# Four groups of z as two 512-wide seven-product units in the front of a hybrid decoder layer

## The chip, the cores and the metric

The kernel runs on one core of a Trainium2 chip. The metric is the device time of one execution in microseconds; lower is better. The core's engines are called PE (TensorE, matmuls), DVE (VectorE), ACT (ScalarE), POOL (GpSimd) and SP (SyncE, which issues the DMAs here). They run side by side, each through its own queue in order, and wait for one another through semaphores.

## The reference

One layer over 1024 tokens of width 1024:

```python
h = rms_norm(x, norm_w)
proj = h @ w_in
q, k, v, z_a, xbc, z_s, dt_raw, gate_logits = jnp.split(proj, SPLIT_POINTS, axis=-1)
...
y_a = diff_attention(...)                  # 8 heads, two softmax maps per head
y_a = y_a * jax.nn.silu(z_a)
xbc = jax.nn.silu(causal_depthwise_conv(xbc, conv_w, conv_b))
...
y_s = ssd_chunked(...)                     # 32 heads in 4 groups, chunks of 128
y_s = gated_group_rms_norm(y_s, z_s, ssd_norm_w)   # group g uses silu of z_s[:, 512 g : 512 g + 512]
merged = sigmoid(g_a) * (y_a @ w_proj_attn) + sigmoid(g_s) * (y_s @ w_proj_ssd)
x = x + (merged @ w_out)
```

The change is in the front: the parts of `h @ w_in` that give z_s (2048 columns, called z below, four groups of 512), xBC (the conv's input, 3072 columns, blocks c0 to c23) and the first gates (g0 to g11).

## The kernel before

**Arithmetic.** All large matmuls are in float32r with each operand split into a high and a low part (h into hH and hL, a weight tile into its two halves w[:, 0] and w[:, 1]). Each product is three matmuls, hi x hi, hi x lo, lo x hi (`steps3`, which calls `mm`, L205). A split is a copy on ACT (`act`, L231) and a subtraction on DVE or POOL (`tt`, L239).

**Seven products.** Most blocks of the projection are multiplied in 2 x 2 halves with seven products instead of eight. With h's halves and weights' halves, the sums of h's parts are the forms t1 to t4 (beside the plain b11, b21, b22), and the sums of the weights' parts are made on POOL. `ORDER` names the seven as (form of h, number of the product): b11 1, t2 6, b21 2, t3 7, t1 5, t4 4, b22 3. Products 1 and 2 go to one PSUM bank, the others to two more; between them DVE and ACT carry partial sums (ct is the copy of product 1, u6 and u7 are that copy plus products 6 and 7).

- `front_pair` does this for two conv blocks or two gates (kinds c and g): weights are stationary, the moving operand is 128 x 512, the banks are fX, fY, fZ. Its step (`conv_step`, `gate_step`, `front_sum`) copies product 1 as fc, makes fu and fW, and sends the result on to conv or gate.
- `tok_unit` does it for one group of z: here the tokens are stationary and the moving operand is a 128 x 256 tile of weights (`tok_w`, `tok_splits`: the tiles rawt, wt, s3), so its matmuls write halves of the banks tx, ty, tz, two of each.
- `ssd_proj_z` makes one group of z plainly, 512 wide. z0 is made this way (`PLAIN`); it runs first, while the tokens' tiles of h come in. `z_evac` applies silu and stores z in DRAM (z_d).
- `form_evac` makes the forms of a token tile (r11, r21 from hH + hL, b12 and b22 copied in `h_evac`), and splits them into sixteen tiles ft, all four forms for a tile after each other. Every product that reads a form waits until all forms of all tiles are made (`("formed", t)`).

**Weights.** `w_loads` issues the loads (raw, rawf, rawt, rawp) in the order of `wlist`, `w_splits` splits them into w, wt or wp; `pair_splits` forms the sums for `front_pair`. For the last product (w_out) `out_sums` makes the sums of the weights' parts beforehand and keeps them in DRAM (wf_d).

**What sets the order.** The source is a set of generators under a planner (`Plan`). It keeps a clock of its own from fixed costs for each operation, and emits instructions in the order that this clock gives; the order on each engine is thus fixed when the kernel is built. `bulk` is the main line, TensorE's large blocks in the order of `FRONT_ORDER`; the other tasks (`ssd_all`, `prepare`, the evacuations) insert their instructions between. `PACE` and `SLOW` are the planner's distances between chunks of the SSD scan. After the front come attention's projections and heads (pma, sc, av, with SSD chunks between), the remaining gates (pg), the products with w_proj (px, py, pz; their forms f0b, f0t, f1b ... are loaded from DRAM in `fill`, their weights as rawp), and the product with w_out (po).

Of the kernel before, what the change touches and what calls it, by code (L numbers as in the profile page):

```python
# [142 lines left out]
def tile_hybrid_layer(ctx: ExitStack, tc: tile.TileContext, x, norm_w, w_in, q_norm_w, k_norm_w,  # L143
# [215 lines left out]
    FPAIRS = [i for i in ORDER1 if i[0] in "cgazv" and i not in PLAIN]  # L359
# [5 lines left out]
    def tok_w(c0):  # L365
        return tuple(w_in[kh * 512 + kp * 256:kh * 512 + kp * 256 + 256, c0 + r * 256:c0 + r * 256 + 256]
                     .rearrange("(k p) c -> p k c", p=P) for kp in range(2) for kh in range(2) for r in range(2))

    PAIR_C = {"c": C_XBC, "g": C_GATE, "a": C_ZA}
    TOK_C = {"z": C_ZS, "v": C_V}  # L370
    for kind, i in ORDER1:
        if kind in PAIR_C:
            wlist.append(pair_w(w_in, 0, PAIR_C[kind] + i * P))
        elif kind in TOK_C and (kind, i) not in PLAIN:
            wlist.append(tok_w(TOK_C[kind] + i * 512))
        elif kind != "setup":
            wlist += att_w(i) if kind == "h" else wide_w(w_in, C_ZS + i * 512) if kind == "z" else block_w(w_in, KB, C_DT, SH)
# [19 lines left out]
    def w_loads(lo, hi):  # L397
        for i in range(lo, hi):
# [15 lines left out]
            if isinstance(wlist[i], tuple) and len(wlist[i]) == 8:  # L414
                ks = yield from pl.get(raws, 4)
                raw = [rpool.tile([P, 2, 256], F32, tag="raw", name=f"rawt{i}{q}") for q in range(4)]
                at = [load(raw[q], wlist[i][q]) for q in range(4)]
                km = yield from pl.get(mids, 4)
                raw += [midt([P, 2, 256], name=f"rawt{i}{q}") for q in range(4, 8)]
                at += [load(raw[q], wlist[i][q]) for q in range(4, 8)]  # L420
                raw_of[i] = (raw, ks, km, at)
                continue
            while i >= len(wlist) - NFIN and ("filled" not in ready or ready.get("out_sums", INF) > pl.t):
                yield pl.t + 0.5
            k = yield from pl.get(raws)
# [24 lines left out]
    def w_splits():  # L450
        for i in range(len(wlist)):
# [5 lines left out]
            if isinstance(wlist[i], list):  # L457
                yield from pair_splits(*raw_of.pop(i), "G" if i < NFRONT else "V")
                continue
            if isinstance(wlist[i], tuple) and len(wlist[i]) == 8:  # L460
                yield from tok_splits(*raw_of.pop(i))
                continue
# [14 lines left out]
            t = tt(lo, raw, hi, ALU.subtract, t, "G" if NW <= i < len(wlist) - NFIN and i % WPOOL == 0 else "V")  # L477
# [5 lines left out]
    def pair_splits(raw, ks, at, eng):  # L483
# [30 lines left out]
        raws.give(ks[0], max(t, t4))  # L514
        t22 = yield from split(a22, at[1], eng)
        t = yield from split(a12, t4, eng)
        raws.give(ks[2], t)
        raws.give(ks[3], max(t, t22))

    def tok_splits(raw, ks, km, at):  # L520

        a11, a21, a12, a22 = [[raw[q], raw[4 + q]] for q in range(4)]
        kt = yield from pl.get(mids, 2)
        s3 = [midt([P, 2, 256], name="s3") for _ in range(2)]

        def split(src, ts, eng):
            done = []
            for kp in range(2):
                k = yield from pl.get(ws)
                n = made[0]  # L530
                made[0] += 1
                wt = wpool.tile([P, 2, 2, 256], F32R, tag="w", name=f"wt{n}")
                yield ts[kp]
                t = act(wt[:, 0], src[kp], AF.Copy, ts[kp])
                yield t
                t = tt(wt[:, 1], src[kp], wt[:, 0], ALU.subtract, t, eng)
                wts[n], w_at[n], w_slot[n] = wt, t, k
                done.append(t)
            return done

        t0 = [max(at[0:4]), max(at[4:8])]
        t3, t1, t2, t4 = [], [], [], []
        for kp in range(2):
            yield t0[kp]
            t3.append(tt(s3[kp], a11[kp], a21[kp], ALU.subtract, t0[kp], "G"))
            t1.append(tt(a21[kp], a21[kp], a22[kp], ALU.add, t0[kp], "G"))
        u11 = yield from split(a11, t0, "V")
        for kp in range(2):
            t2.append(tt(a11[kp], a21[kp], a11[kp], ALU.subtract, max(t1[kp], u11[kp]), "G"))
        yield from split(a11, t2, "V")  # L550
        u12 = yield from split(a12, t0, "V")
        for kp in range(2):
            t4.append(tt(a12[kp], a12[kp], a11[kp], ALU.subtract, max(t2[kp], u12[kp]), "G"))
        raws.give(ks[0], t4[0])
        mids.give(km[0], t4[1])
        t = yield from split(s3, t3, "G")
        for kp in range(2):
            mids.give(kt[kp], t[kp])
        t = yield from split(a21, t1, "V")
        raws.give(ks[1], t[0])  # L560
        mids.give(km[1], t[1])
        t = yield from split(a22, t0, "G")
        raws.give(ks[3], t[0])
        mids.give(km[3], t[1])
        t = yield from split(a12, t4, "G")
        raws.give(ks[2], t[0])
        mids.give(km[2], t[1])
# [96 lines left out]
    def load_x(t):  # L664
# [626 lines left out]
    def tok_step(kind, g, p, b, bank, cell):  # L1291
# [4 lines left out]
        def out(src, o, k, at, free):  # L1296
# [5 lines left out]
            if free:  # L1302
                trs.give(kb, at)
# [892 lines left out]
```

## Time and profile before

| what | value |
|---|---|
| median of 3 runs (lowest to highest) | 1588.59 us (1586.92 to 1589.97) |
| profiled execution | 1586.5 us |
| its span | 1584.8 us |
| granted clock | 0.999 |
| PE busy | 1564.0 us, 8386 instructions |
| DVE, ACT, POOL busy | 1153.5, 939.0, 787.8 us |
| DMA | 247.56 MB, mean 156 GB/s |

The span is the stretch from the first to the last instruction of the profiled execution. A stretch such as 40 to 80 is in microseconds from its start. The front takes the first 580 us or so, attention lasts to about 1210, the last gates to 1260, the products to 1500, and w_out the rest. In rows of groups the columns are line, engine, operation, out<-in with shape and count, then busy us and mean ns of one, then the idle time before it and who ended it. In the chain of waits the columns are start, length, and what ran.

### The profile page before, as it was taken

To read this page: it belongs to the slowest core of one execution; us is meant where nothing else is said; L and a number is where in the kernel's file an instruction comes from. 1 tells how busy PE (TensorE), PEld (TensorE's weight loads), DVE (VectorE), ACT (ScalarE), POOL (GpSimd) and SP (SyncE) were. 2 spreads that over 40 slices of the span, in tenths; PEclk is the share of its full clock that TensorE was granted. 3 is DMA by queue.
4 is the path that set the end of the run, shared out by engine and by line. 5 is a ranking of instruction groups with operands and counts; after the bars stand their busy time and mean duration, and the time that the engine had idled before them with its cause. 6 is when DMAs were issued, how large, how long until landed. Compare 5 with 4: busy or idle time off the path is not lost.

```text
span 1584.8 us, 25484 instructions
## 1 busy us (share of the span) xinstructions
PE 1564.0 (99%) x8386; PEld 1330.4 (84%) x8386; DVE 1153.5 (73%) x2104; ACT 939.0 (59%) x2267; POOL 787.8 (50%) x909
## 2 busy tenths in 40 slices
PE   8999999999999999999999999999999999999999
PEld 6898889888988888888888888888888878888887
DVE  7967664777567666877777788776566677898985
ACT  8544456665475466777787777686566554443350
POOL 3554455554654533546594646445747664322005
PEclk9999999999999999999999999999999999999999
DMA  5233344345343461415273442324426787898846
GB/s 183 94 110 87 120 153 127 100 134 169 104 137 118 144 196 45 127 54 159 84 239 115 144 117 88 105 73 131 166 89 226 237 302 239 273 318 277 305 139 219
DMA packets 236006, 247.56 MB, mean 156 GB/s; under 512 B 15959, under 2 KB 168288, under 8 KB 235874
## 3 DMA queue, kind: packets, MB, share of 16 engines
q1 hardware_dynamic: 235870, 245.94, 48.5%
q8 instruction: 66, 1.08, 0.3%
q14 instruction: 66, 0.54, 0.1%
q10 hardware_dynamic: 4, 0.00, 0.0%
HBM read 172.35 MB, written 73.53 MB: 155 GB/s over the span
## 4 chain that ended last, share of the span: by engine, by line
PE 71%; ACT 4%; POOL 2%; DVE 1%; DMA 1%; issue 1%; SPq 0%; DVEq 0%; POOLq 0%; ACTq 0%
PE pma L205 18%; PE py L205 6%; PE sc L205 4%; PE pO L205 4%; PE av L205 4%; PE px L205 4%; PE pz L205 4%; PE fYc L205 3%; PE pg L205 3%; PE fXc L205 2%; PE pa L214 2%; PE fZc L205 2%; PE fYg L205 2%; PE poz L205 1%; PE fZg L205 1%; PE poy L205 1%
## 5 line engine op out<-in xcount | busy, mean ns | idle before, releaser
L205 PE MATMUL pma<-w,hH 128*128 128x512 f32 x1024 | 342.3, 403 | 1.9 <-POOL w L239 1.7
L205 PEld LDWEIGHTS pma<-w,hH 128*128 128x128 f32 x1024 | 187.9, 189 | 35.1 <-POOL w L239 2.1
L205 PE MATMUL pma<-w,hL 128*128 128x512 f32 x512 | 206.9, 404 | 0.0
L239 POOL TENSOR_TENSOR rawf<-rawf,rawf 128x512 f32<-128x512 f32 x54 | 70.5, 1306 | 116.4 <-DVE wp L239 42.9
L231 ACT ACTIVATE p<-p,nm 128x256 f32<-128x256 f32 (+7 forms) x128 | 98.7, 774 | 26.9 <-DVE nm L941 21.5
L205 PEld LDWEIGHTS pma<-w,hL 128*128 128x128 f32 x512 | 96.6, 189 | 16.0
L205 PE MATMUL fYc<-ft,wp 128*128 128x512 f32 x432 | 105.0, 390 | 0.0
L231 ACT ACTIVATE w<-raw 128x512 fp32r<-128x512 f32 (+1 forms) x110 | 67.4, 626 | 49.0 <-DMA raw<-wf_d 12.8
L205 PEld LDWEIGHTS fYc<-ft,wp 128*128 128x128 f32 x432 | 80.9, 188 | 16.7
L231 ACT ACTIVATE wp<-rawf 128x512 fp32r<-128x512 f32 x108 | 64.8, 624 | 44.2 <-POOL rawf L239 19.7
L231 ACT ACTIVATE wp<-rawp 128x512 fp32r<-128x512 f32 x72 | 44.1, 627 | 76.7 <-POOL rawp L239 18.7
L231 ACT ACTIVATE ab<-ab,nac 128x128 f32<-128x128 f32 x256 | 78.5, 397 | 7.0 <-POOL ab L1450 6.8
L239 DVE TENSOR_TENSOR w<-raw,w 128x512 fp32r<-128x512 f32 (+1 forms) x85 | 68.2, 816 | 18.0 <-ACT w L231 17.6
L239 POOL TENSOR_TENSOR rawp<-rawp,rawp 128x512 f32<-128x512 f32 x36 | 54.4, 1528 | 52.0 <-DVE wp L239 43.7
L941 DVE CUSTOM_DVE_ANT_0 p<-sc,maskb 128x512 f32<-128x512 f32 (+3 forms) x128 | 72.3, 583 | 7.9 <-PE sc L205 7.1
L205 PEld LDWEIGHTS av<-v,at 128*128 128x128 f32 x576 | 72.5, 191 | 4.9 <-ACT at L231 1.3
L271 POOL TENSOR_TENSOR rs<-rs,mhalf 128x4 f32<-128x4 f32 (+1 forms) x71 | 73.3, 1033 | 5.9
L205 PE MATMUL av<-v,at 128*128 128x128 f32 x576 | 74.7, 275 | 0.5 <-ACT at L231 0.5
L973 POOL TENSOR_TENSOR rec<-s,mone 128x1 f32<-128x1 f32 x64 | 35.7, 560 | 74.8 <-ACT p L231 74.7
L205 PE MATMUL sc<-kk,qh 128*128 128x512 f32 (+2 forms) x192 | 66.7, 353 | 0.6 <-ACT ch L231 0.4
L239 DVE TENSOR_TENSOR wp<-rawf,wp 128x512 fp32r<-128x512 f32 x72 | 56.5, 798 | 14.8 <-ACT wp L231 14.8
L205 PE MATMUL fXc<-hH,wp 128*128 128x512 f32 x192 | 63.9, 392 | 0.0
(383 smaller groups left out, 4585.6 us busy)
## 6 DMA issues: line engine op xcount, KB each, us to landing
raw<-in_w_in_dram SPq DMA_DIRECT2D x80, 256.0 KB, 3.6
rawf<-in_w_in_dram SPq DMA_DIRECT2D x72, 256.0 KB, 3.4
ab<-act_d SPq DMA_DIRECT2D x32, 512.0 KB, 4.2
cv_d<-cv SPq DMA_DIRECT2D x48, 256.0 KB, 2.3
t_d<-ts SPq DMA_DIRECT2D x24, 512.0 KB, 2.7
xr<-cv_d SPq DMA_DIRECT2D x32, 256.0 KB, 3.5
zc<-z_d SPq DMA_DIRECT2D x32, 256.0 KB, 3.4
ys_d<-xdt SPq DMA_DIRECT2D x32, 256.0 KB, 2.5
```

Of the source, the lines that this page charges most:

```text
L205: nc.tensor.matmul(o, lhsT=lhsT, rhs=rhs, start=start, stop=stop, **kw)
L214: nc.tensor.transpose(out=o, in_=i, identity=ident if idn is None else idn)
L231: nc.scalar.activation(o, i, f, **kw)
L239: (nc.vector if eng == "V" else nc.gpsimd).tensor_tensor(out=o, in0=a, in1=b, op=op)
L271: nc.gpsimd.tensor_tensor(out=dst, in0=dst, in1=mhalf[:, 0:cols], op=ALU.pow)
L941: nc.vector.tensor_tensor_reduce(out=p[:, j:e], in0=sc[i][:, 0:e - j], in1=maskb[:, S - n + j:S - n + e], scale=-1.0, scalar=nms[i - 1] if ...
L973: nc.gpsimd.tensor_tensor(out=rec, in0=sums[1], in1=mone, op=ALU.pow)
```

## The change

- **z in two units of two groups.** `z_first` ("y0", "y1") computes, 512 wide and plainly, the token tiles 0 to 3 of groups 0 and 2 (products 1 and 2). After half of the sum ACT copies the bank (zc) and the copy goes to DRAM (zc_d); PE then adds the second half into the same bank. `z_part` ("z06", "z17": unit, product) does one of the five remaining products over four token tiles with 512-wide moving weights (banks pz); its partial sums (zu, zv) are loaded from DRAM and stored back, unless the next block of the order is a part of the same unit. The parts stand between other blocks.
- **Weight sums in DRAM.** `weight_sums` makes the four sums of a unit's weights on POOL from tiles os and stores them in wf_d, at the planner's times `ZSUMS`; the loads of z's parts read them from there, and wait until they are stored (`gate`). It also serves w_out in place of `out_sums`.
- **Four gates begun apart.** "e6", "e0", "e4", "e2" (`gate_first`) do products 1 and 2 of a gate pair (its first block, the first half of the tokens): half of the sum, copy by ACT (gc, kept in gc_d), the other half. The pair's remaining five products come later in the order `REST`, with the copy loaded as fc.
- **Forms one by one.** `form_evac` makes t2 for all token tiles, then t3 and t1, then t4; a product waits for its own form only (`formed`). b12 and b22 lie in one large tile (b2).
- **Numbers.** PACE 19.5 (19), SLOW 32 (40), POOL takes every third weight split only from i = 48 (`NEARLY`) and not from 9; the order of the front is another.

In all the program has 7280 large matmuls of the projections' kind in place of 7808 (1008 of 256 columns fall away, 480 of 512 come), 2145 DVE instructions in place of 2106, 2044 on ACT in place of 2038, 911 on POOL in place of 914, and SP issues 1068 DMAs in place of 916.

```diff
-PACE = 19
-FRONT, SLOW = 12, 40.0
-FRONT_ORDER = "z0 d0 z1 c16 c20 g0 c0 c2 g2 z2 c4 c6 g4 c18 c22 g6 z3 c8 c10 g8 c12 c14 g10"
-PLAIN = (("z", 0),)
+PACE = 19.5
+FRONT = 12
+SLOW = 32.0
+FRONT_ORDER = "y0 e6 y1 e0 e4 c6 e2 d0 c20 z06 c16 z07 z05 g0 c2 z04 c0 z16 z03 g2 z17 z15 z14 c4 z13 c8 g8 c14 g6 c22 g10 c12 g4 c10 c18"
+REST = (("t2", 6), ("b22", 3), ("t3", 7), ("t1", 5), ("t4", 4))
+ZSUMS = (75.0, 182.0, 11.0)
 WPOOL = 3
+NEARLY = 48
...
+    wf_d = dram.tile([12, 2, P, S], F32, name="wf_d")
+    gc_d = dram.tile([2048, 512], F32, name="gc_d")
+    zc_d = dram.tile([2, 2, 512, 512], F32, name="zc_d")
...
+    def blocks_w(src, c0, sums, p, kb):
+        if p in (1, 2, 4):
+            i, j = {1: (0, 0), 2: (1, 0), 4: (1, 1)}[p]
+            return src[(i * 4 + kb) * P:(i * 4 + kb + 1) * P, c0 + j * 512:c0 + (j + 1) * 512]
+        j, h = {6: (0, 0), 7: (0, 1), 3: (1, 0), 5: (1, 1)}[p]
+        return wf_d[sums * 4 + kb, j][:, h * 512:(h + 1) * 512]
...
+            while i in gate and ready.get(gate[i], INF) > pl.t:
+                yield pl.t + 0.2
...
-            t = tt(lo, raw, hi, ALU.subtract, t, "G" if NW <= i < len(wlist) - NFIN and i % WPOOL == 0 else "V")
+            t = tt(lo, raw, hi, ALU.subtract, t, "G" if NEARLY <= i < len(wlist) - NFIN and i % WPOOL == 0 else "V")
...
+    def formed(f, ts=range(4, NT)):
+        while any(("formed", f, t) not in ready for t in ts):
+            yield pl.t + 0.2
+        at = max(ready["formed", f, t] for t in ts)
+        if at > pl.t:
+            yield at
...
-                while any(("formed", t) not in ready for t in range(4, NT)):
-                    yield pl.t + 0.2
-                at = max(ready["formed", t] for t in range(4, NT))
-                if at > pl.t:
-                    yield at
+                yield from formed(f)
...
+    def gate_first(b):
+        ids = w_next(2)
+        k = yield from pl.get(trs, first=True)
+        pm = mmt(f"pe{b}")
+        for half in range(2):
+            yield from w_need(ids[half])
+            while half and ("g", b) not in g_c:
+                yield pl.t + 0.1
+            for kb in range(half * 4, half * 4 + 4):
+                yield from steps3(pm, blk(ids, kb), (hH[:, kb, 0:512], hL[:, kb, 0:512]), kb == 0, kb % 4 == 3, skip_group_check=True)
+            w_done(ids[half])
+            if half:
+                pl.spawn(gate_evac(b, 0, pm, k), pe_done())
+            else:
+                pl.spawn(gate_copy(b, pm), pe_done())
...
+    def gate_copy(b, pm):
+        at = pe_done()
+        km = yield from pl.get(mids)
+        c = midt(name=f"gc{b}")
+        at = act(c, pm, AF.Copy, at)
+        g_c["g", b] = at
+        yield at
+        g_c["g", b] = at = load(gc_d[b * P:(b + 1) * P], c, at)
+        mids.give(km, at)
...
+    def z_first(pr):
+        ids = w_next(KB)
+        for ts in (((0, 1), (2, 3)) if pr else ((0,), (1,), (2, 3))):
+            pms = []
+            for t in ts:
                 k = yield from pl.get(trs, first=True)
+                pms.append((mmt(f"pmz{pr}{t}"), k))
+            for half in range(2):
+                for t, (pm, k) in zip(ts, pms):
+                    while half and (pr, t) not in z_c:
                         yield pl.t + 0.1
+                    for kb in range(half * 4, half * 4 + 4):
+                        yield from w_need(ids[kb])
+                        while (t, half) not in h_at:
+                            yield pl.t + 0.1
+                        while h_at[t, half] > pl.t:
+                            yield h_at[t, half]
+                        yield from steps3(pm, hblk(kb, t), wide(ids[kb]), kb == 0, kb % 4 == 3, skip_group_check=True)
+                        if t == 3:
+                            w_done(ids[kb])
+                    pl.spawn(z_evac(2 * pr, t, pm, k, False) if half else z_copy(pr, t, pm), pe_done())
...
+    def z_copy(pr, t, pm):
         at = pe_done()
+        km = yield from pl.get(mids)
+        c = midt(name=f"zc{pr}{t}")
+        at = act(c, pm, AF.Copy, at)
+        z_c[pr, t] = at
+        yield at
+        z_keep(pr, 0, t, c, km, at, False)
...
+    def z_part(pr, p, keep):
+        f, ids = FORM_OF[p], w_next(4)
+        for t in range(4):
+            k = yield from pl.get(trs, first=True)
+            pm = trt(f"pz{p}{pr}{t}")
+            if f[0] == "t":
+                yield from formed(f, (4 + t,))
+            us = {}
+            pl.spawn(z_fetch(pr, p, t, us))
+            for kb in range(4):
+                yield from w_need(ids[kb])
+                yield from steps3(pm, [a[:, t * P:(t + 1) * P] for a in front_form(f, kb)], wide(ids[kb]), kb == 0, kb == 3)
+                if t == 3:
+                    w_done(ids[kb])
+            pl.spawn(z_step(pr, p, t, pm, k, us, keep), pe_done())
...
+    def z_step(pr, p, t, pm, k, us, keep):
+        at = pe_done()
+        while len(us) < 1 + (p == 5):
+            yield pl.t + 0.1
+        yield max([at] + [u[2] for u in us.values()])
+        at = pl.t
+        if p == 6:
+            c, km = us[0][0:2]
+            at = tt(c, c, pm, ALU.add, at)
+            trs.give(k, at)
             yield at
+            z_keep(pr, 0, t, c, km, at, keep)
...
+    def weight_sums(n, src, c0, at=0.0):
+        yield at
+        for kb in range(4):
+            ks = yield from pl.get(mids, 4)
+            a, b = [[midt(name=f"os{n}{kb}{j}{i}") for i in range(2)] for j in range(2)]
+            t = max(load((a, b)[j][i], src[(j * 4 + kb) * P:(j * 4 + kb + 1) * P, c0 + i * 512:c0 + i * 512 + 512])
+                    for j in range(2) for i in range(2))
+            yield t
+            for p, x, k, o, y, z, op in ((5, b[1], 3, b[1], b[1], a[1], ALU.add), (7, a[1], 1, a[1], a[0], a[1], ALU.subtract),
+                                         (6, a[0], 0, a[0], b[1], a[0], ALU.subtract), (3, b[0], 2, b[0], b[0], a[0], ALU.subtract)):
+                yield from pl.room("G")
+                t = tt(o, y, z, op, t, "G")
+                pl.spawn(sum_store(n, kb, p, x, ks[k], t))
+                if p == 3:
+                    ready["summed", n, kb] = t
+                t -= HOP
...
-        for kind, i in ORDER1:
+        step = {"y": z_first, "h": att_proj, "e": gate_first}
+        for i in range(2):
+            pl.spawn(weight_sums(i, w_in, C_ZS + i * 1024, ZSUMS[i]))
```

Three places show how the order moves. On PE in the startup (ph are transposes of x, pmz the banks of z's token tiles; a w is one weight tile) there stands before, at the middle of the first tile's sum:

```order
L214 MATMUL ph_234<-ident,x_142 128x128 [waits DVE_49]
L214 MATMUL ph_234<-ident,x_142 128x128 x3
L205 MATMUL pmz_144<-w_172,hH 128x512
L205 MATMUL pmz_144<-w_172,hL 128x512
L205 MATMUL pmz_144<-w_204,hH 128x512 [waits Activation_49]
```

and now the same bank's second half, w_212 to w_248, waits for ACT, whose queue is, from the first tile's hH halves to the copy of the second tile's bank (zc_364):

```order
L234 ACTIVATE hH<-ph_242 128x4x128 [waits PE_49]
L234 ACTIVATE zc_257<-pmz_144 128x512 [waits PE_49]
L234 ACTIVATE hL,ss<-x_192 128x8x128 [waits DMAHW5_49]
L234 ACTIVATE hL,ss<-x_194 128x8x128 [waits DMAHW6_49]
L234 ACT_TABLE_LOAD
L234 ACTIVATE zs_287<-pmz_144 128x512 [waits PE_49]
L234 ACTIVATE hL,ss<-x_196 128x8x128 [waits DMAHW7_49]
L234 ACTIVATE hL,ss<-x_198 128x8x128 [waits DMAHW0_49]
L234 ACTIVATE hH<-ph_318 128x4x128 [waits PE_49]
L234 ACTIVATE hL,ss<-x_200 128x8x128 [waits DMAHW1_49]
L234 ACTIVATE hH<-ph_347 128x4x128 [waits PE_49]
L234 ACTIVATE zc_364<-pmz_285 128x512 [waits PE_49]
```

The wait of w_204 was for its own weight split; the wait of w_212 is also for zc_257, and that of the second tile for zc_364, with squares (hL,ss) and h halves ahead of it.

On DVE, the last splits of form t4 (ft_518 and ft_519 before, ft_906 and ft_907 now; r are the form's sums) stood before the splits of the first weights that any product with a form reads (wt):

```order
L239 TENSOR_TENSOR ft_518<-r_529,ft_516 128x2x128 [waits Activation_49,Pool_49]
L239 TENSOR_TENSOR ft_514<-b_486,ft_512 128x2x128 [waits Activation_49]
L239 TENSOR_TENSOR wt_769<-rawt_683,wt_769 128x512 [waits DMAHW5_49,PE_49,Activation_49]
L239 TENSOR_TENSOR wt_773<-rawt_722,wt_773 128x512 [waits DMAHW2_49,PE_49,Activation_49]
L239 TENSOR_TENSOR ft_518<-r_583,ft_516 128x2x128 [waits Activation_49]
```

and now they stand inside block c6 (fu, fW are its partial sums, fYc and fZc its banks):

```order
L242 TENSOR_TENSOR fu_1036<-fc,fYc_939 128x512 [waits DMAHW3_49,PE_49]
L242 TENSOR_TENSOR w_1041<-raw_1008,w_1041 128x512 [waits DMAHW5_49,Activation_49]
L242 TENSOR_TENSOR w_1057<-raw_1010,w_1057 128x512 [waits DMAHW6_49,Activation_49]
L242 TENSOR_TENSOR w_1063<-raw_1022,w_1063 128x4x32 [waits DMAHW7_49,Activation_49]
L242 TENSOR_TENSOR fW_1070<-fu_1036,fZc_940 128x512 [waits DVE_49,PE_49]
L242 TENSOR_TENSOR w_1068<-raw_1031,w_1068 128x4x32 [waits DMAHW0_49,Activation_49]
L242 TENSOR_TENSOR ft_906<-r_746,ft_904 128x2x128
L242 TENSOR_TENSOR ft_907<-r_746,ft_905 128x2x128
L242 TENSOR_TENSOR ft_906<-r_728,ft_904 128x2x128
L242 TENSOR_TENSOR ft_907<-r_728,ft_905 128x2x128
```

The last two token tiles' halves of t4 come after fW, which waits for PE's last matmul of product 5; product 4, next on PE, reads them.

On SP, at the start of the products (f0b are the rows of y_s that the first products read, rawp their weights), before:

```order
L260 DMA f0b_14771<-ys_d 128x512
L260 DMA f0b_14787<-ys_d 128x512
L260 DMA rawp_14793<-in_w_proj_ssd_dram 128x4x128
L260 DMA rawp_14794<-in_w_proj_ssd_dram 128x4x128
L260 DMA rawp_14813<-in_w_proj_ssd_dram 128x4x128
L260 DMA f0b_14836<-ys_d 128x512
L260 DMA f0b_14841<-ys_d 128x512
```

and now:

```order
L263 DMA f0b_14426<-ys_d 128x512
L263 DMA f0b_14433<-ys_d 128x512
L263 DMA os_14491<-in_w_out_dram 128x512
L263 DMA f0b_14504<-ys_d 128x512
L263 DMA f0b_14510<-ys_d 128x512
L263 DMA f1b_14516<-ys_d 128x512
L263 DMA rawp_14605<-in_w_proj_ssd_dram 128x4x128
L263 DMA rawp_14633<-in_w_proj_ssd_dram 128x4x128
```

The eight rawp loads (the first and last of them shown) stood between the first and the last two f0b loads, and stand behind all four now.

More of the change, by code (lines that the diff above doesn't have):

```diff
@@ L413, in w_loads @@
                 continue
[L414 to L423, printed above, removed]
+            while i >= len(wlist) - NFIN and ("filled" not in ready or ready.get((2, 3, 3), INF) > pl.t):
                 yield pl.t + 0.5
+            while i in gate and ready.get(gate[i], INF) > pl.t:
+                yield pl.t + 0.2
             k = yield from pl.get(raws)
@@ L513, in pair_splits @@
         raws.give(ks[1], max(t, t2))
-        raws.give(ks[0], max(t, t4))
+        raws.give(ks[0], max(t, t4, s2))
         t22 = yield from split(a22, at[1], eng)
[L516 to L567, printed above, removed]
@@ L569, in pairs_splits @@
+        raws.give(ks[3], max(t1, t22))
+        if not short:
+            t = yield from split(a12, t4, eng)
+            raws.give(ks[2], t)
     def pairs_splits(raw, ks, at, late):
@@ L853, in att_proj, with h_done @@
                 qk = []
+    def h_done():
+        yield pl.t + 5.6
+        for k in range(2 * KB):
+            hs.give(k, pl.t)
     def hblk(kb, t):
@@ L1178, in front_pair @@
     def front_pair(kind, b, last):
-        ids = w_next(7)
+        rest = (kind, b) in g_c
+        order = REST if rest else ORDER
+        ids = w_next(len(order))
         ks = []
@@ L1183, in front_pair @@
         x, y, z = trt(f"fX{kind}{b}"), mmt(f"fY{kind}{b}"), trt(f"fZ{kind}{b}")
-        into = {1: x, 6: y, 2: x, 7: y, 5: z, 4: y, 3: z}
+        into = {1: x, 6: y, 2: x, 7: y, 5: z, 4: y, 3: x if rest else z}
         cell = {"kc": (yield from pl.get(mids)), "x": x, "ks": ks}
+        if rest:
+            cell["c"] = midt(name="fc")
+            cell["ct"] = load(cell["c"], gc_d[b * P:(b + 1) * P], g_c[kind, b])
         if kind == "c":
@@ new lines, in z_copy, with z_keep, z_get @@
+    def z_copy(pr, t, pm):
+        at = pe_done()
+        km = yield from pl.get(mids)
[4 more added lines that the diff above has]
+        z_keep(pr, 0, t, c, km, at, False)
+    z_u = {}
+    def z_keep(pr, n, t, o, km, at, keep):
+        if not keep:
+            at = load(zc_d[pr, n, t * P:(t + 1) * P], o, at)
+            mids.give(km, at)
+            o = None
+        z_u[pr, n, t] = (o, km, at)
+    def z_get(pr, n, t):
+        while (pr, n, t) not in z_u:
+            yield pl.t + 0.1
+        o, km, at = z_u.pop((pr, n, t))
+        stored = o is None
+        if stored:
+            km = yield from pl.get(mids)
+            o = midt(name=f"zu{pr}{n}{t}")
+            at = load(o, zc_d[pr, n, t * P:(t + 1) * P], at)
+        return o, km, at, stored
@@ new lines, in z_back @@
+    def z_back(pr, n, t, u, keep, at):
+        if keep or not u[3]:
+            z_keep(pr, n, t, *u[0:2], max(at, u[2]), keep)
+        else:
+            mids.give(u[1], at)
+            z_u[pr, n, t] = (None, None, at)
+    FORM_OF = {p: f for f, p in ORDER}
+    def z_part(pr, p, keep):
[13 more added lines that the diff above has]
+            pl.spawn(z_step(pr, p, t, pm, k, us, keep), pe_done())
@@ L1713, in prepare_a, with sum_store @@
+    def sum_store(n, kb, p, x, k, t):
+        yield t
+        j, h = {6: (0, 0), 7: (0, 1), 3: (1, 0), 5: (1, 1)}[p]
+        ready[n, kb, p] = t = load(wf_d[n * 4 + kb, j][:, h * 512:(h + 1) * 512], x, t)
+        while p == 6 and ("summed", n, kb) not in ready:
+            yield pl.t + 0.2
+        mids.give(k, max(t, ready["summed", n, kb]) if p == 6 else t)
     def prepare_a():
```

321 lines of the change are left out of this document (126 added, 195 removed).

## The prediction

> **What bounds the kernel now.** I read the head of the page first, then the stretches of the span, then the chain that ended last.
>
> ```profile
> PE 1564.0 (99%) x8386; PEld 1330.4 (84%) x8386; DVE 1153.5 (73%) x2104; ACT 939.0 (59%) x2267; POOL 787.8 (50%) x909
> PE 71%; ACT 4%; POOL 2%; DVE 1%; DMA 1%; issue 1%; SPq 0%; DVEq 0%; POOLq 0%; ACTq 0%
> ```
>
> TensorE is busy 99% of the span and holds 71% of the chain. No other engine comes near; so only two things can move the end: fewer or cheaper matmuls, and pauses of PE. The stretches (length, then busy time of PE, PEld, DVE, ACT, POOL, then clock, DMA share, GB/s) tell where the pauses lie now:
>
> ```profile
> 0.00:40.00 40.00, 34.62 (x158) 25.77 (x159) 28.32 (x49) 32.71 (x60) 15.72 (x32) 1.00 0.54 181
> 40.00:80.00 40.00, 40.00 (x213) 32.21 (x212) 38.55 (x57) 20.28 (x52) 22.93 (x15) 1.00 0.28 93
> 160.00:280.00 120.00, 119.67 (x702) 106.29 (x702) 69.65 (x109) 64.09 (x118) 64.67 (x51) 1.00 0.43 134
> 280.00:420.00 140.00, 138.79 (x711) 117.67 (x711) 107.15 (x174) 81.66 (x159) 72.65 (x61) 1.00 0.40 122
> 420.00:560.00 140.00, 138.97 (x763) 120.29 (x762) 93.25 (x151) 80.94 (x159) 71.89 (x63) 1.00 0.46 138
> 600.00:1280.00 680.00, 674.63 (x3849) 577.28 (x3848) 494.93 (x1075) 478.97 (x1398) 393.10 (x575) 1.00 0.42 134
> 1280.00:1320.00 40.00, 36.34 (x166) 29.84 (x165) 29.21 (x40) 17.74 (x34) 19.36 (x14) 0.96 0.72 231
> ```
>
> The front (z, conv, gates), which the change rewrites, has almost nothing to win in pauses: from 160 to 560 PE idles 0.33 + 1.21 + 1.03 = 2.57 us. But ACT is busy 32.71 of the first 40 us and DVE 38.55 of the next 40: new waits on these two are paid in full there.
>
> **The matmuls.** The chain gives the issue rate of both widths, the groups the number of narrow ones (tx, ty, tz are the banks of z's token units):
>
> ```profile
> 345.11 2.72 PE fXc L205 x12
> 416.36 5.76 PE txz L205 x48
> 442.36 2.88 PE tzz L205 x24
> 1313.66 5.44 PE px L205 x24
> ...
> L205 PE MATMUL tyz<-wt,ft 128*128 128x256 f32 x432 | 55.2, 284 | 0.0
> L205 PE MATMUL txz<-wt,hH 128*128 128x256 f32 x192 | 35.0, 283 | 0.0
> L205 PE MATMUL txz<-wt,hL 128*128 128x256 f32 x96 | 27.3, 285 | 0.0
> L205 PE MATMUL tzz<-wt,ft 128*128 128x256 f32 x144 | 18.3, 284 | 0.0
> L205 PE MATMUL tzz<-wt,hH 128*128 128x256 f32 x96 | 17.7, 284 | 0.0
> L205 PE MATMUL tzz<-wt,hL 128*128 128x256 f32 x48 | 13.7, 284 | 0.0
> ```
>
> A 512-wide matmul is issued every 5.44/24 = 0.2267 us, a 256-wide one every 5.76/48 = 0.1200, 6% more per column. The six groups are 1008 matmuls: 121.0 us. In their place stand five products of 48 matmuls for each of two units, 480 x 0.2267 = 108.8 us. The 192 plain matmuls of z0 become 96 + 96 of y0 and y1, and the gates' 7 products keep their number. **Term 1: -12.1 us**, of which 24 x 0.2267 = 5.4 is fewer columns and 6.7 the width. The mean durations (284) overlap and are no price.
>
> [...]
>
> **Copies of a half-made bank.** y and e stop after half of their sum; ACT copies the bank, and PE's next matmul into the same bank waits for that copy. The trace has this round trip once bare, and what ACT does in the startup:
>
> ```profile
> 500.31 0.58 ACT L231 ACTIVATE fc<-fXg 128x512 f32<-128x512 f32 x1
> 500.94 0.50 PE L205 MATMUL fXg<-hH,wp 128*128 128x512 f32 x1 [1.03 <-ACT fc L231]
> ...
> L231 ACT ACTIVATE hH<-ph 128x512 fp32r<-128x512 f32 x16 | 8.8, 605 | 0.9 <-PE ph L214 0.9
> L231 ACT ACTIVATE hL<-x 128x1024 fp32r<-128x1024 f32 (+1 forms) x9 | 8.7, 965 | 0.8 <-DMA x<-in_x_dram 0.8
> L231 ACT ACTIVATION_READ_ACCUMULATOR hL<-x 128x1 f32 x9 | 1.7, 194 | 0.0
> ```
>
> Bare, PE loses 1.03. e0, e4 and e2 have nothing else between the halves: **term 2: 3 x 1.0 = +3.0**. In the startup four such waits stand (y0's tile 0, tile 1, the pair 2 and 3, and e6), where ACT serves its queue in order: the copy of tile 0 stands behind two hH copies (1.2), that of tile 1 behind three squares (3 x 1.16) and four hH copies, which partly wait for PE's own transposes. Worked along the queue, they lose about 1.5, 3.0, 1.7 and 0.9. All four bare give 4.0; all four as bad as tile 1 give 12.0. I take **term 3: +5.5**, nearer the bare ones, since the pair has twelve matmuls of the other bank to hide its wait and e6 comes when ACT has thinned out. y1 works in pairs and costs nothing; its cover is the twelve matmuls of the other tile (2.7 us).
>
> **Forms made one by one.** Before, all sixteen form tiles were split ahead of the first product that read one. Now c6 reads t4 right after t1, and on DVE six operations stand between PE's last t1 matmul and the second t4 matmul:
>
> ```profile
> L239 DVE TENSOR_TENSOR fW<-fu,fZc 128x512 f32<-128x512 f32 x12 | 8.3, 692 | 7.6 <-PE fZc L205 7.5
> L239 DVE TENSOR_TENSOR w<-raw,w 128x128 fp32r<-128x128 f32 x1 | 1.3, 1319 | 0.0
> L239 DVE TENSOR_TENSOR ft<-r,ft 128x256 fp32r<-128x256 f32 x16 | 11.7, 772 | 0.0
> L239 DVE TENSOR_TENSOR ft<-b,ft 128x256 fp32r<-128x256 f32 x16 | 9.3, 622 | 1.0 <-ACT ft L231 1.0
> ...
> 81.47 1.28 ACT L231 ACT_TABLE_LOAD   x1
> 82.76 0.42 ACT L231 ACTIVATE tv<-tv 128x256 f32<-128x256 f32 x1
> 83.77 1.75 DVE L1112 RECIPROCAL tv<-tv 128x256 f32<-128x256 f32 x1
> L239 DVE TENSOR_TENSOR tv<-tv,tv 128x256 f32<-128x256 f32 x1 | 0.9, 870 | 0.0
> ```
>
> fW 0.69 can start only when PE's fZc is done; then come a 128-wide weight split (1.3 in the trace, where DVE shared its time with other work; by its size nearer 0.3) and three form halves of 0.62 to 0.77, the last of which PE needs: 2.9 to 4.3, less the first matmul's 0.23. **Term 4: +3.2** (0 if the halves get done ahead of fW, 4.1 at most). A delay of PE elsewhere doesn't help, as the row of operations starts at PE's own matmul.
>
> The dt chain moves beside c20: table load 1.28, exp 0.42, reciprocal 1.75, a product 0.87 stand on ACT and DVE ahead of fu, which must read bank fY before c20's product 7 goes into it. From product 1's end: fc's copy 1.0, these four 4.3, two smaller operations on the same tile (some 1.3, an estimate between the 0.42 and the 0.87), fu 0.7: 7.3, against the 5.4 us of products 6 and 2 (24 matmuls). Before, the chain lay beside z1's unit, which had two of each bank. **Term 5: +2.0** (0 to 3).
>
> **What else moves.** POOL makes 32 more weight sums, and SP issues 152 more DMAs (sums and partial z out to DRAM and back, some 36 MB):
>
> ```profile
> L239 POOL TENSOR_TENSOR os<-os,os 128x512 f32<-128x512 f32 x16 | 22.9, 1429 | 7.9 <-DMA os<-in_w_out_dram 4.5 <-PE av L205 2.4 <-DVE y L247 0.5
> raw<-in_w_in_dram SPq DMA_DIRECT2D x80, 256.0 KB, 3.6
> zc<-z_d SPq DMA_DIRECT2D x32, 256.0 KB, 3.4
> ```
>
> 32 x 1.43 = 46 us on a POOL that is half idle from 160 to 420 hides there, as do 36 MB at a DMA share of 0.4 (the startup moved 181 GB/s at 0.54); the z parts fetch their partial sums a product (2.7 us) ahead, a landing takes 3.4. The first part (z06) reads weight sums that were stored shortly before, and can wait some tenths. **Term 6, small waits of the new front: +1.0** (-2 to 4; -2.57 would be all of the idle time above).
>
> Behind the front, attention and the products keep their order but stand some us earlier against the queues. Its idle time is 680.00 - 674.63 = 5.4 us, spread widely; **term 7: -1.0** (-2 to 1), as fewer groups of instructions crowd between two matmuls there. The products' start is plainer:
>
> ```profile
> PE py L205 <- DVE u L239: 3.7, 1, 3.7
> 1294.57 5.73 DMA f0b<-ys_d
> 1303.56 4.62 PE py L205 x12
> ```
>
> SP issues eight rawp loads ahead of two f0b loads; u, behind the f0b split on DVE, frees PE 3.7 us late, and the next twelve matmuls take 4.62 instead of 2.72, 1.9 more. Now the four f0b loads stand ahead of the rawp loads. Up to 5.6 can come back; **term 8: -3.5**, as ACT and DVE still have wp and f0b splits to do there.
>
> Sum: -12.1 + 3.0 + 5.5 + 3.2 + 2.0 + 1.0 - 1.0 - 3.5 = **-1.9**. The profiled execution took 1586.5 (span 1584.8), 2.1 under the median 1588.59; as a difference the sum is applied to the median: **1586.7**. A difference under 0.2% (3.2 us) counts as none.
>
> **Rivals.** (a) The waits are absorbed: the four copies cost the bare 4.0, e's 3.0, t4 1, dt 0.5, the rest 0, the products -4, attention -1: -12.1 + 3.5 = -8.6, 1580. For it speaks that PE ran from 40 to 80 with no pause beside a DVE at 38.55 of 40; against it that what terms 2 to 4 wait for starts at PE's own last matmul. With every bound at its best (t4 and dt 0, products -5.5, attention -2) it is -12.6: 1576. (b) The startup queue: each of the four copies waits as tile 1's, 12.0 instead of 5.5, since ACT, at 32.71 of 40, gets five more copies: sum +4.6, 1593. It decides as soon as the four cost over 10.6. (c) The products' pause stays, since SP's 7.69 us of rawp loads only moves: +3.5, sum +1.6, 1590.2. (d) The narrow matmuls were no dearer per column in their place, so that only the 24 fewer count: gain 5.4 instead of 12.1, sum +4.8, 1593.4; every row of the two widths speaks against it. [...]
>
> A wait of 3.66 us was followed by a slower clock (0.96 in the stretch from 1280). [...]
>
> **Chances.** The sum 0.42, its own range 1583 to 1591: 0.10 faster, 0.27 same, 0.05 slower. (a) 0.29, faster. (b) 0.17, slower. (c) 0.09: 0.05 same, 0.04 slower. (d) 0.03, slower. Together faster 0.39, same 0.32, slower 0.29. The range goes from 1576 (every bound at its best) to 1597: (b) with (c)'s 3.5, +8.1.
>
> **What would show it.** pz matmuls at 5.44 per 24 show term 1. The waits of PE should name ACT zc and gc (together 7 to 10 us), one long wait of fYc on DVE ft near 100 us, one on DVE fu near 125 us; py on u should shrink below 2, and 1303's slow dozen vanish. A list of PE waits without zc and ft makes (a) true; zc alone over 10 us makes (b). Long PE waits on raw or zu loads would show DMA as a cost that I hold to be hidden, and prove me wrong.

## The result and the profile after

| | before | after |
|---|---|---|
| median | 1588.42 us (1586.92 to 1589.97) | 1580.01 us (1579.40 to 1582.61) |
| profiled execution's span | 1584.8 us | 1578.7 us |

The ratio is 0.9950, 95% interval 0.9933 to 0.9967: the change is 8.4 us faster (5.2 to 10.6). A second comparison of the same two kernels gave 1579.11 against 1588.82, ratio 0.9941 (0.9926 to 0.9956). The forecast of 1586.7 missed by 6.7 us, within its range of 1576 to 1597.

The head of the page after:

```profile
PE 1553.7 (98%) x7858; PEld 1299.0 (82%) x7858; DVE 1183.6 (75%) x2143; ACT 939.4 (60%) x2273; POOL 785.3 (50%) x906
```

Its stretches, with the columns as before (length, busy time of PE, PEld, DVE, ACT, POOL, clock, DMA share, GB/s):

```profile
0.00:40.00 40.00, 31.32 (x135) 22.95 (x136) 25.33 (x42) 30.61 (x57) 14.94 (x31) 0.96 0.65 224
40.00:80.00 40.00, 38.58 (x171) 31.30 (x170) 30.30 (x53) 25.59 (x55) 9.49 (x7) 1.00 0.53 168
80.00:160.00 80.00, 75.24 (x334) 57.82 (x333) 64.09 (x103) 35.56 (x70) 46.52 (x36) 1.00 0.68 217
160.00:280.00 120.00, 120.00 (x531) 99.26 (x530) 87.13 (x134) 51.55 (x93) 66.23 (x50) 1.00 0.83 275
600.00:1280.00 680.00, 677.86 (x3879) 581.31 (x3878) 497.11 (x1085) 482.72 (x1409) 394.21 (x577) 1.00 0.42 136
1280.00:1320.00 40.00, 38.91 (x172) 31.91 (x171) 32.94 (x39) 17.86 (x32) 23.69 (x16) 1.00 0.83 283
```

Before, the third of these read:

```profile
80.00:160.00 80.00, 80.00 (x486) 71.91 (x485) 55.49 (x87) 36.21 (x62) 39.79 (x32) 1.00 0.34 98
```

PE has 528 matmuls fewer (7858 for 8386) and, from 40 to 160, 6.2 us of idle time where it had none. From 600 to 1280 it idles 2.1 us instead of 5.4, and the stretch from 1280 has its full clock. Among the waits of PE (engine, line, waited for: total, times, longest) are all that the prediction named, zc, gc, ft, fu and u; a selection:

```profile
PE pmz L208 <- ACT zc L234: 4.3, 2, 2.9
PE pe L208 <- ACT gc L234: 2.9, 4, 0.7
PE fYc L208 <- DVE ft L242: 1.8, 1, 1.8
PE pO L208 <- POOL wp L242: 1.4, 1, 1.4
PE py L208 <- DVE u L242: 1.1, 1, 1.1
PE fYc L208 <- DVE fu L242: 0.7, 1, 0.7
```

To compare stages I sum, over PE's matmuls, the distance from start to start beyond the usual one of that kind of matmul (its median before); these are its pauses. What is left is its work, which is thus the number of matmuls of each kind times the usual distance, and the same in both profiles of a kernel; all that differs from one execution to the next lies in the pauses. The rows leave out 7.2 to 7.5 us of the span, mostly the time before the first matmul and after the last. "Attention" goes from the first pma to the first product with w_proj, the last gates within. Both kernels have two profiles:

| us | before | before again | after | after again |
|---|---|---|---|---|
| work of PE | 1545.0 | 1545.0 | 1532.8 | 1532.8 |
| pauses 0 to 40 | 6.6 | 6.5 | 11.3 | 9.3 |
| pauses of the front from 40 | 5.3 | 5.5 | 14.6 | 15.4 |
| pauses of attention | 14.9 | 15.1 | 11.1 | 10.7 |
| pauses of the products | 5.7 | 7.3 | 1.4 | 1.4 |
| span | 1584.8 | 1586.6 | 1578.7 | 1577.0 |

The front alone thus gained nothing: 12.2 us less work, 13.4 us more pauses (means of the two pairs), 1.2 us lost. What the change brought stands behind the front: 4.1 us in attention and 5.1 at the products' start, 8.0 in all after the front's loss.

### The profile page after: what moved, and what is told of

The parts are those of the page before. It is cut to its first block, busy times and chain, and to the rows that moved or that the text cites. A ratio compares the mean times of both kernels' runs of the same rounds, so it can differ in the third digit from the quotient of the medians.

```text
span 1578.7 us, 24834 instructions
## 1 busy us (share of the span) xinstructions
PE 1553.7 (98%) x7858; PEld 1299.0 (82%) x7858; DVE 1183.6 (75%) x2143; ACT 939.4 (60%) x2273; POOL 785.3 (50%) x906
## 4 chain that ended last, share of the span: by engine, by line
PE 85%; ACT 3%; DVE 3%; DMA 3%; POOL 3%; issue 2%; SPq 0%; POOLq 0%; DVEq 0%; ACTq 0%
PE pma L208 19%; PE pz L208 11%; PE py L208 5%; PE fYc L208 5%; PE sc L208 4%; PE pO L208 4%; PE av L208 4%; PE fXc L208 3%; PE fZc L208 3%; PE px L208 3%; PE fYg L208 3%; PE pg L208 2%; PE pmz L208 2%; PE pa L217 2%; PE poz L208 1%
## 5 line engine op out<-in xcount | busy, mean ns | idle before, releaser
L234 ACT ACTIVATE w<-raw 128x512 fp32r<-128x512 f32 (+1 forms) x166 | 101.3, 629 | 56.0 <-DMA raw<-wf_d 21.7
L242 DVE TENSOR_TENSOR w<-raw,w 128x512 fp32r<-128x512 f32 (+1 forms) x134 | 107.1, 817 | 27.0 <-ACT w L234 24.1
L208 PE MATMUL pz<-w,ft 128*128 128x512 f32 x384 | 90.1, 391 | 0.9 <-DVE w L242 0.9
L242 POOL TENSOR_TENSOR os<-os,os 128x512 f32<-128x512 f32 x48 | 66.9, 1393 | 36.4 <-DMA os<-in_w_in_dram 14.8
L208 PEld LDWEIGHTS pz<-w,ft 128*128 128x128 f32 x384 | 71.7, 188 | 16.0 <-DVE w L242 1.3
L234 ACT ACTIVATE wp<-rawf 128x512 fp32r<-128x512 f32 x100 | 60.5, 624 | 17.5 <-POOL rawf L242 16.3
```

Of the source, the lines that this page charges most:

```text
L208: nc.tensor.matmul(o, lhsT=lhsT, rhs=rhs, start=start, stop=stop, **kw)
L234: nc.scalar.activation(o, i, f, **kw)
L242: (nc.vector if eng == "V" else nc.gpsimd).tensor_tensor(out=o, in0=a, in1=b, op=op)
```

## Experiments

**The two kernels again** (unchanged).

> The changed kernel once more, for a second profile. If the pauses of PE in the two profiles are a property of the program, attention (from the first pma to the first pg, with the gates behind it) again shows some 11 us of pauses, the startup's two waits on zc again 1.6 and 3.1, and the time is 1579 to 1583. If attention's 3.8 us of gain was chance of one execution, its pauses lie nearer the 14.9 of before.

> The kernel before once more, for a second profile: is the 3.66 us wait of py at 1303 with the slow dozen behind it (1.9), and are attention's 14.9 us of pauses, there again? If they belong to the program, all come back within 1 us; if chance, attention differs by 2 or more.

Measured: 1579.11 us and, in a single execution, 1588.29 us, pauses as in the table. Attention's and the products' pauses belong to the programs; the profiles of one program agree there within 0.4 us, but for py's wait (3.66, then 4.75). The startup differs by 2 us between two executions of one program.

**The width alone.** First with the planner left to itself:

```diff
-                yield from steps3(pm, [a[:, t * P:(t + 1) * P] for a in front_form(f, kb)], wide(ids[kb]), kb == 0, kb == 3)
+                for c in range(2):
+                    yield from steps3(pm[:, c * 256:c * 256 + 256], [a[:, t * P:(t + 1) * P] for a in front_form(f, kb)],
+                                      [v[:, c * 256:c * 256 + 256] for v in wide(ids[kb])],
+                                      kb == 0 and c == 0, kb == 3, skip_group_check=True)
```

> The changed kernel with each 512-wide matmul of z's five products (480) made as two 256-wide ones (960), nothing else. If a narrow matmul costs 0.120 us, as before's rows say, this is 960 x 0.1200 - 480 x 0.2267 = +6.4 us against the changed kernel, 1586 to 1587, and the width alone carries half of the change's 12.1. [...]

Measured: 1616.48 us, 37 above the changed kernel. PE's work rose by 6.2 us (1539.0), as the rows' 0.120 us has it, but attention's pauses rose from 11 to 25.5 and the products' from 1.4 to 12.6: the planner's clock ran differently from z's first part on, and everything behind stood in another order. So the same edit with the clock held:

```diff
+                    was = pl.t
+                    for c in range(0, 512, 256):
+                        nc.tensor.matmul(pm[:, c:c + 256], lhsT=x, rhs=y[:, c:c + 256], start=kb + m + c == 0,
+                                         stop=kb == 3 and m == 2, skip_group_check=True)
+                    pl.t = was + 512 / 2400 + lag[0]
```

> The changed kernel with the same 960 narrow matmuls in place of z's 480 wide ones, but the planner's clock still charged for the wide ones, so that every engine keeps its order. [...]

Measured: 1586.94 us, ratio to before 0.9989 (0.9979 to 0.9998), against 0.9941 and 0.9950 of the changed kernel: 6 to 8 us slower, where PE's work had risen by 6.2 in the first try. The order on every engine is that of the changed kernel, and the front's pauses are 16.3. The chain of waits has the same run of matmuls in both, first in the changed kernel, then in this one:

```profile
177.09 21.76 PE pz L208 x96
```

```profile
176.95 23.03 PE pz L1356 x192
```

That is 0.2267 us for a wide matmul and 0.1199 for a narrow one, 1.27 us for a fifth of the 480, so 6.3 for all. The width's half of term 1 is thereby shown.

**Pacing.** `PACE` 19 to 19.5 and `SLOW` 40 to 32 in the kernel before, and the other way round in the kernel after:

> The kernel before with PACE 19.5 and SLOW 32 alone, so that the SSD chunks are spaced as in the changed kernel. If attention's gain of 3.8 us comes from this spacing, its pauses fall from 14.9 towards 11 and the time by 2 to 4. If it comes from the front's other end and weight order, nothing moves by more than 1.5.

> The changed kernel with PACE 19 and SLOW 40, the numbers of before. If these numbers only move some SSD chunks, the time is within 4 us of the changed kernel's; if each order of the front needs its own numbers, as the 32 us of before with 19.5 and 32 suggest, single waits of 3 us and more of PE appear between 300 and 620 and it is 5 to 30 us slower, and may lose the whole gain.

Measured: 1620.46 us, 32 slower than before, and 1603.62, 24 slower than after. The first was expected to move by 4 us at most, which was far off; for the second, 5 to 30 us slower was one of the two cases expected. The two longest waits of PE in the first:

```profile
PE pO L205 <- DVE cv L247: 6.5, 1, 6.5
PE py L214 <- ACT xn L231: 5.7, 2, 5.4
```

PE's work is the same; its pauses in the front are 36.9 instead of 5.3. In the second they are 22.7 in the front and 29.0 in attention. Each of the two orders lost by the other's pair of numbers, and attention's pauses rose in the first too, by 1.7 us; so the pacing by itself is not what made attention faster.

**The copies of tiles 0 and 1 on DVE**, all else in place (the planner is charged as for ACT):

```diff
-        at = act(c, pm, AF.Copy, at)
+        at = act(c, pm, AF.Copy, at, on=pr == 0 and t < 2)     # on: nc.vector.tensor_copy
```

> The changed kernel with the copies of y0's tiles 0 and 1 made by DVE instead of ACT, the planner's clock charged as before, so that every other instruction keeps its place. If the two waits on zc (1.6 and 3.1 us) are ACT's queue (squares and h halves ahead of the copy), they fall to about the bare 0.9 each, and the startup's pauses by some 2.5 us, the time by 2 to 3. If they are the price of the round trip itself or DVE is as crowded, nothing moves by more than 1.

Measured: 1581.18 us (ratio 0.9961, 0.9946 to 0.9975): no gain, where 2 to 3 us were expected. Its waits of PE:

```profile
PE fYc L208 <- DVE fu L245: 1.9, 1, 1.9
PE pmz L208 <- DVE zc L235: 1.2, 1, 1.2
PE pmz L208 <- ACT zc L237: 0.9, 1, 0.9
PE pmz L208 <- ACT hL L237: 0.9, 1, 0.9
```

ACT's queue was the cause of the long wait: tile 1's wait of 2.9 (2.3 in the second profile) became 0.9. The list puts it down to hL, a square on ACT that ended just behind DVE's copy. Tile 0's wait only went from 1.4 (1.8) to 1.2. The startup's pauses fell to 8.1, of which 0.7 to 0.9 us came from a shorter wait on x ahead of all copies. But the pair's copy, still on ACT, now waits 0.9 as well, and at 132 us fu was 1.9 late instead of 0.7: the front's pauses rose to 18.3. Gained 1 to 3 us, given back 3 to 4.

**Where the products' pause comes from.** In the kernel before, the last two f0b loads from ACT's DMA queue, and in another kernel one f0b split on POOL, all else in place:

```diff
+                    t = load(form[0][:, 1].bitcast(F32), src, eng=nc.scalar if (c, f) == (0, "b22") and i > 1 else None)
...
+        t = yield from split_in_place(form, t, "G" if (c, f, i) == (0, "b22", 2) else None)
```

> The kernel before with the last two f0b loads of product b22 issued from ACT's queue instead of SP's, so that they don't stand behind the eight rawp loads; all else keeps its place. If that queue is the cause of py's wait, the wait of 3.7 to 4.8 us at 1303 and the slow dozen behind it (1.9) shrink to under 2 together and the kernel gains 4 to 5 us, which is what the changed kernel gains there. If DVE's own work (the f0b and wp splits) is the cause, 3 us or more stay.

> The kernel before with one split of f0b (product b22, third tile) on POOL instead of DVE, everything else in its place. Between PE's last py matmul and the u that frees py, DVE ran pc, a wp split and this f0b split (0.69 + 0.68 + 1.69). [...] If the wait has another cause, 3 us or more stay.

Measured: 1587.47 (ratio 1.0001, 0.9991 to 1.0010) and, in a single execution, 1586.56 us; py still waits 3.8 and 3.4 us for u, so in both the expectation of 3 us or more came true. DVE in order of time in the first:

```profile
1300.32 0.69 DVE L239 TENSOR_TENSOR pc<-pc,py 128x512 f32<-128x512 f32 x1 [3.43 <-PE py L205]
1300.93 0.82 DVE L239 TENSOR_TENSOR wp<-rawp,wp 128x512 fp32r<-128x512 f32 x1
1301.67 1.75 DVE L239 TENSOR_TENSOR f0b<-f0b 128x512 fp32r<-128x512 f32 x1
1303.34 0.68 DVE L239 TENSOR_TENSOR u<-pc,py 128x512 f32<-128x512 f32 x1
```

and DVE and PE in the second, where the chain of waits has the store that u waited for below:

```profile
1300.93 0.69 DVE L239 TENSOR_TENSOR wp<-rawp,wp 128x512 fp32r<-128x512 f32 x1
1302.92 0.69 DVE L239 TENSOR_TENSOR u<-pc,py 128x512 f32<-128x512 f32 x1 [1.31 <-DMA wf_d<-os]
1303.67 1.20 PE L205 MATMUL py<-hL,wp 128*128 128x512 f32 x3 [3.38 <-DVE u L239]
```

```profile
1298.03 4.80 DMA wf_d<-os
```

Two things end within 0.5 us of each other. With the loads out of the way, DVE still runs a wp and an f0b split between pc and u. With the f0b split gone, u waits for its buffer, which a store of weight sums (wf_d) still reads until 1302.83. Each alone covers the other. In the changed kernel DVE has done the f0b splits by 1290, and only one split (f1t, 1.77) stands right ahead of u (DVE and PE in order of time):

```profile
1296.63 1.77 DVE L242 TENSOR_TENSOR f1t<-f1t 128x512 fp32r<-128x512 f32 x1
1298.33 0.67 DVE L242 TENSOR_TENSOR u<-pc,py 128x512 f32<-128x512 f32 x1
1299.06 0.96 PE L208 MATMUL py<-hH,wp 128*128 128x512 f32 x3 [1.09 <-DVE u L242]
```

Removing both in the kernel before wasn't tried; that the two together make the pause, and that the changed kernel is rid of it for this reason, is read from the traces and not shown by a run.

**One wait of attention.** In the kernel before, pma waited 1.7 us at 912 for a weight split on POOL; that split (w69) on DVE, all else in place:

> The kernel before with one weight split, w69, on DVE instead of POOL, the planner's clock charged for POOL. It is the split that pma waited 1.7 us for at 912. If attention's gain is the sum of single waits of this kind, this one goes away and attention's pauses fall from 14.3 to about 12.5, with the rest as it was; if it is the whole stretch's alignment, another wait takes its place and the sum stays above 13.8.

Measured, in a single execution: 1587.26 us. The wait is gone, attention's own pauses (without the last gates) fell from 14.3 and 14.4 to 13.5: half of it came back in small waits (pq on a DVE qk, 0.5, is new). Between the two expectations; the rest of attention's 4.1 us stays open, spread over waits of under 1 us.

**Two repairs of the changed kernel.** e0 and e4 made together, and c6 put behind e2:

```diff
-    def gate_first(b):
+    def gate_first(bs):      # halves of all banks in turn: "e0 e4" is called with [0, 4]
...
-... e0 e4 c6 e2 d0 ...
+... e0 e4 e2 c6 d0 ...
```

> The changed kernel with the gates e0 and e4 made together, so that the copy of one bank lies beside twelve matmuls of the other. Two of the four waits of 0.9 on gc go, -1.8 us; what follows is ordered anew by the planner. If the rest keeps its pauses, it is 1577 to 1579; if a new order costs more than such a wait, it is slower than the changed kernel.

> The changed kernel with the block c6 behind e2 instead of ahead of it, so that t4's last splits lie beside e2's 24 matmuls. The wait of fYc on ft (1.9 us at 104) goes, if DVE's row of fW, a weight split and three form halves is its cause; the time falls by 2 if the planner's new order has no other wait of that size, and rises if it has.

Measured: 1587.38 us (ratio 1.0003, 0.9994 to 1.0013) and 1603.60 (1.0107, 1.0088 to 1.0127). In the first, gc waits twice instead of four times, but 3.0 us in total as before (2.9), since one wait is now 2.3 long; in the second no wait on ft is left. The new orders brought other waits, the case in which each expectation had a slower kernel. The first:

```profile
PE pe L208 <- ACT gc L234: 2.3, 1, 2.3
PE pz L208 <- DVE w L242: 2.1, 1, 2.1
```

The front's pauses are 22.3 and 27.9 instead of 15. No version here beat the changed kernel.

## Why the prediction was right or wrong

The measured time lies at rival (a)'s 1580, but that is chance: (a) lets the front's waits be absorbed (8.5 us left of them), and they were not (13.4). The sum's own mechanism was right in the front, and its terms behind the front were too small. Of the 6.1 us between the sum (-1.9) and the stages' difference (-8.0), term 7 makes 3.1, term 8 1.6, and terms 2 to 6 together 1.3.

- **Term 1** (-12.1): right, -12.2 by the table's count; the width's part is shown by the kernel with narrow matmuls in the same order. Rival (d) doesn't hold for these matmuls: 0.1199 us for a narrow one is more than half of the wide one's 0.2267.
- **Term 2** (+3.0): 2.7. Each of e0, e4 and e2 costs 0.90, of which the copy gc is 0.6, as the chain of waits shows for the last:

```profile
112.26 0.61 ACT gc L234
112.91 3.03 PE pe L208 x12
```

- **Term 3** (+5.5): in the first profile 1.6 + 3.1 + 0 + 0.85 = 5.5. The four waits that the prediction worked out add up to 7.1 (1.5, 3.0, 1.7, 0.9), and it took 5.5, as the pair had another bank's matmuls to hide its wait. The pair indeed didn't wait at all, and e6's wait was bare, as said. The chain of waits shows tile 1's copy behind the squares (hL) and the h halves, in the order worked out:

```profile
20.10 1.28 ACT L234
21.40 0.60 ACT zs L234
22.00 2.07 ACT hL L234 x4
24.07 0.97 ACT hH L234 x2
25.04 1.03 ACT hL L234 x2
26.07 0.97 ACT hH L234 x2
27.05 0.50 ACT zc L234
```

  The first two rows, a table load and zs, stand in the same queue without a gap, and the working of 3.0 doesn't count them. Their 1.9 us is most of what this wait has over a bare one, so its agreement (3.1) is in part chance.

- **Term 4** (+3.2): the wait is there, at 1.9. The row of operations was right, their durations not: the four form halves took 1.42 together, the narrow split 0.28, where the rows of the groups had means of 0.62 to 0.77 and 1.3.

```profile
101.98 0.69 DVE L242 TENSOR_TENSOR fW<-fu,fZc 128x512 f32<-128x512 f32 x1 [0.30 <-PE fZc L208]
102.58 0.28 DVE L242 TENSOR_TENSOR w<-raw,w 128x128 fp32r<-128x128 f32 x1
102.78 1.42 DVE L242 TENSOR_TENSOR ft<-r,ft 128x256 fp32r<-128x256 f32 x4
103.93 2.35 PE L208 MATMUL fYc<-ft,wp 128*128 128x512 f32 x9 [1.76 <-DVE ft L242]
```

  The means mix two durations: most halves take about 0.41 or about 1.51 us (before, four at 61.93 took 1.42 together, two at 66.14 took 2.95). In the two kernels' traces the long ones (8 of 32 before, 7 of 32 after) all ran beside a busy POOL, for 1.23 us or more of their time, though not every half beside a busy POOL is long: at 61.93 it was busy, too (61.47 to 64.50). At 102.78 POOL was idle. The narrow split's 1.3 before (1.32 at 29.87) ran beside a busy POOL as well (sums r, 28.51 to 33.59). Why some are long was not tested.

- **Term 5** (+2.0): 0.8, the dt chain as described (table load, exp, reciprocal, fu at 132.3). From product 1's end to fu's end it took 6.0 us and not 7.3, as the small operations and fc's copy were shorter than put down.
- **Term 6** (+1.0): what remains of the front's pauses is about +2.5: 1.2 on a weight split of z06's product, 1.5 on POOL's wp at 477, 1.0 each at 448 and 565. The added DMA cost nothing that PE's waits show, at 275 GB/s and a share of 0.83 from 160 to 280. Together terms 2 to 6 were 14.7; the pauses up to attention rose by 14.0 in the first pair of profiles and by 12.7 in the second. That the total came so near is partly luck: terms 4 and 5 were 2.5 us too high, and term 6 was 1.5 too low.
- **Term 7** (-1.0, bounds -2 to 1): the step that failed most, -4.1. The bounds were drawn from idle time alone and from a feeling for how instructions crowd. The trace of before listed single waits in attention (1.7 on w alone), and the prediction didn't ask of each whether the new order would keep it. Which part of the change took most of them away stays open.
- **Term 8** (-3.5): -4.3 to -5.9. The size was near; the cause given, SP's row of loads, was not it: with two of the f0b loads out of that row the wait stayed. By the traces, DVE's splits ahead of u and a buffer held by a store end together.
- The first profile of before was 1.9 us faster than its median and 1.8 faster than the second profile, which hid part of the difference: py's wait was 3.66 and 4.75, and the products' pauses 5.7 and 7.3.

Rival (b) didn't come, as the copies cost 5.5 and not over 10.6, and (c) didn't, as the products' pause went.

## What to carry over

Where one engine is busy 99% of the time, a wait that begins at its own last instruction can be placed by hand, by following the other engine's queue from that instruction: all the waits came where they were named, though single terms were off by up to 1.5 us, and the total of 13 to 14 us for 14.7 owes something to errors that cancel. What is far behind the change can't be left at "about the same" when a planner orders everything: moving two pacing numbers, or narrowing matmuls, cost 24 to 37 us, so an effect of one edit is measured only with the order held. And a cause with a twin behind it shows nothing when it is removed alone; look at what would be late next before crediting it.

## What was new about the hardware

A wait of PE of only 1.35 us was followed by a clock of 0.50 for 3.41 us; one of 1.37 us in the same place was not. It is the wait on POOL's wp in two executions of the changed kernel, in order of time, the second profile first:

```profile
474.50 1.97 PE L208 MATMUL pO<-xdt,ab 128*128 128x64 f32 x16 [1.35 <-POOL wp L242]
```

```profile
477.33 1.97 PE L208 MATMUL pO<-xdt,ab 128*128 128x64 f32 x16 [1.37 <-POOL wp L242]
```

In the first profiles of the two kernels the clock is 0.50 in one stretch of 3.41 us each, 27.22 to 30.63 after and 1304.12 to 1307.53 before; from there it is 1.00 for 453 and 81 times 3.413 us, up to 0.50 again at the very end (from 1576.87 and 1584.01). In the second profile of the changed kernel it is 0.50 from 476.43 to 479.84. The rows below are stretches of 3.41 us laid out from these steps: those that hold the two waits, and those behind them, in the second profile and then in the first (columns as above: PE's busy time comes second, the clock is the third number from the end):

```profile
473.02:476.43 3.41, 2.06 (x18) 1.96 (x18) 2.59 (x4) 0.78 (x1) 1.39 (x2) 1.00 0.60 165
476.43:479.84 3.41, 3.41 (x10) 2.67 (x10) 3.33 (x7) 0.75 (x2) 0.00 (x0) 0.50 0.86 226
```

```profile
474.36:477.77 3.41, 2.04 (x12) 1.45 (x11) 3.41 (x6) 0.66 (x1) 2.88 (x2) 1.00 0.43 115
477.77:481.18 3.41, 3.41 (x23) 3.07 (x23) 2.51 (x5) 1.18 (x2) 0.00 (x0) 1.00 0.90 261
```

And for the startup's long wait on zc, 2.31 us in the second profile and 2.91 in the first:

```profile
22.46:25.87 3.41, 2.15 (x16) 1.57 (x13) 2.52 (x4) 3.41 (x8) 1.86 (x6) 1.00 0.96 313
25.87:29.28 3.41, 2.36 (x12) 2.00 (x13) 3.41 (x7) 3.01 (x7) 1.71 (x4) 1.00 0.11 34
29.28:32.69 3.41, 3.41 (x22) 2.91 (x21) 3.38 (x6) 2.52 (x6) 3.41 (x3) 1.00 0.12 27
```

```profile
23.81:27.22 3.41, 0.87 (x6) 0.43 (x4) 3.20 (x5) 3.41 (x9) 1.75 (x5) 1.00 0.46 166
27.22:30.63 3.41, 3.04 (x10) 2.45 (x10) 3.41 (x7) 1.87 (x4) 1.89 (x3) 0.50 0.13 39
```

After 1.35 us the clock was 0.50, after 1.37 it stayed at 1.00; after 2.31 it stayed, after 2.91 it was 0.50. The stretches fall differently on the program in the two executions. The 2.31 us are divided between two of them, with 2.15 and 2.36 us of PE's work. Of the 2.91 most fall into one, with 0.87 us of work. The two short waits leave PE equally busy (2.06 and 2.04), but where the clock was halved 16 of the 18 matmuls are pO's, 64 columns wide, and in the other most are 512 wide. So in these four cases the length of the wait alone doesn't sort the halved clocks from the others. This is read from the traces; no run varied it.

In other profiles py's waits of 3.38, 3.66, 3.8 and 4.75 us (before_f0b_pool, before, before_f0b, rep_before) were each followed by a dozen matmuls that took 4.61 or 4.62 us, where a dozen usually takes 2.72. In the kernel with narrow matmuls in the same order PE waited 1.33 us on POOL's wp, and the matmuls behind it started 0.43 us apart (485.74 to 486.17), as the halved ones of the second profile do (476.71 to 477.14). The halved clock from 27.22 in one execution of the changed kernel, and its absence there in the other, is one reason for the startup's 2 us between executions of one program (pauses of 11.3 and 9.3).
